# Seven block products in place of eight for the gate and up matmuls of a streaming encoder layer

## The chip, the cores and the metric

The kernel runs on one core of one Trainium2 chip, in one launch. The metric is the device time of that launch in microseconds. A core has a matrix engine (TensorE, PE in the profile, with its weight loads as PEld), a vector engine (VectorE, DVE), a scalar engine (ScalarE, ACT), a general engine (GpSimd, POOL) and a sync engine (SyncE, SP) that here issues the DMAs. Matmul results go to eight PSUM banks; everything else lies in on-chip memory of 128 partitions.

## The reference

One inference step of one layer with 1024 new tokens of a prompt and 32 tokens of a running stream, 1056 columns in all, model width 1024, feed-forward width 2816. Attention and retention come first; the part that this change touches is the second half:

```python
x = x + mix @ w_o
h = rmsnorm(x, g_ffn)
x = x + (jax.nn.silu(h @ w_ff_gate) * (h @ w_ff_up)) @ w_ff_down
gate = jax.nn.sigmoid(rmsnorm(x, g_ple) @ w_ple_gate)
return x + gate * (p @ w_ple)
```

All data is 32-bit float. Each matmul operand is split into two 16-bit halves (a high part and a rest), and a product is made of three 16-bit matmuls: high by high, high by rest, rest by high.

## The kernel before, in words

Tokens lie along the free dimension, channels along the partitions. The first stage (projections, attention, retention) is planned by hand (class Flow, line 80): a planner with a cost for each step and engine writes out the order. At its end it loads the weights of the output projection (`load_wo_0`, `load_wo_1`, lines 1216 and 1225) and of the last stage's `p @ w_ple` (`load_ple`, 1241), queued at lines 1347 to 1350.

From line 1390 on the order is not written out by hand. The build places each instruction in its engine's queue by dependences and estimated times, with a preference for what comes first in the program; on the chip each queue is then worked off in order. The stages are:

- **Output projection** (1432 to 1461): three token chunks of 352 (`CH`), eight output blocks of 128 channels each, 24 matmuls of 352 columns for each (`mm3`, lines 440 to 443: three matmuls for each of eight input blocks). DVE adds the old x (1451), SP stores it to DRAM (1453), ACT and DVE sum its squares (354). After a chunk `norm_steps` (319) queues three steps that run behind the next products: nothing, then four small matmuls with a power of -1/2 on POOL (333), then the broadcast matmul on PE (342) and the split of the normalized chunk into halves (347 to 352; every second subtraction is on POOL).
- **Gate and up** (1398 to 1430 and 1465 to 1511): 22 rows j of 128 feed-forward channels. `load_gu` brings the gate and the up weights of two rows (1 MB each), finds their largest magnitude (1406 on DVE, then `partition_all_reduce` on POOL, 285), derives a power-of-two scale, and splits them into halves (1410 on ACT, 1411 on DVE). `gu_mm` makes, for each row and each chunk of 352 tokens, a gate and an up product of 24 matmuls each. `gu_out` (1471) makes silu(gate) times up out of the two banks: tanh on ACT (1474), two DVE operations (1475, 1476), a 16-bit copy on ACT (1478), a DVE rest (1479). All 22 result rows stay on the chip in `aT` (1469).
- **Down** (1481 to 1561): eight output blocks m; `load_dn` loads and prepares the weights of one block (its maximum also goes through POOL, 1494), `down` makes 66 matmuls of 352 columns for each token chunk.
- **Last stage** (1564 to 1589): the second norm, the gate product and the output.

PSUM after line 1390: seven rotating banks for the products (`psb`) and one for the norms (`pss`). Weight tiles rotate through three buffers (`wpool`), staged weights through two (`stg`).

Of the kernel before, what the change touches and what calls it, by code (L numbers as in the profile page):

```python
# [33 lines left out]
NCH = 3  # L34
EPS = 1e-6
# [8 lines left out]
def _f(x):  # L44
    return float(x)
# [132 lines left out]
def kernel(  # L178
# [35 lines left out]
    mix_d = dram.tile([H, P, 2, T], F16, name="mix_d")  # L214

# [62 lines left out]
    def weight_scale(amax, n, gi, tag, pool=True, norm=False):  # L278
# [3 lines left out]
        if pool:  # L282
            yield G(0, 0.1)
            ar = sm(n, tag + "ar", 3)
            nc.gpsimd.partition_all_reduce(ar, amax, P, ABSMAX)  # L285
            yield from p2of(p2, ar, n, tag)
        else:
            ar = yield from spread_max(amax, n, tag)
            yield from p2of(p2, ar, n, tag, norm)
            yield ("put", "o")  # L290
# [4 lines left out]
        nc.vector.tensor_scalar(out=s, in0=s, scalar1=_f(2.0 ** -50) if norm else 16384.0, scalar2=None, op0=ALU.mult)  # L295
# [8 lines left out]
    def weight_scale_now(amax, n, gi, tag):  # L304
        g = weight_scale(amax, n, gi, tag)
# [13 lines left out]
    def norm_steps(acc, dg, tag, split, late=0):  # L319

        pending.extend([lambda: None] * late)
        B = CH // 4
        box = []

        def first():
            ps = pss.tile([P, 512], F32, tag="ss", name="ss")
            for b in range(4):
                nc.tensor.matmul(out=ps[0:B, CH + b:CH + b + 1], lhsT=acc[:, b * B:(b + 1) * B], rhs=ones32[:, 0:1],
                                 start=True, stop=True)
            v = sm(4, tag + "v")  # L330
            nc.vector.tensor_scalar(out=v[0:B], in0=ps[0:B, CH:CH + 4], scalar1=_f(1.0 / D), scalar2=EPS, op0=ALU.mult, op1=ALU.add)
# [8 lines left out]
        def second():  # L340
            ps, d = box
            nc.tensor.matmul(out=ps[:, 0:CH], lhsT=ones32[0:B], rhs=d[0:B], start=True, stop=True)
            split(ps[:, 0:CH])
# [10 lines left out]
    def square_sum(pool, xf, k0, k1, acc):  # L354

        for k in range(k0, k1):
            sq = acc if k == 0 else pool.tile([P, CH], F32, tag="sq", name="sq")
# [97 lines left out]
    with ExitStack() as pa:  # L455
# [83 lines left out]
        def const_b():  # L539
# [10 lines left out]
            yield ("delay", 2.0)  # L550

# [760 lines left out]
        def stream():  # L1312
# [10 lines left out]
            for s in range(NT * H + LAG):  # L1323
                at[0] = s
                h, i = divmod(s, NT)
                if h < H:
# [19 lines left out]
                    if i == 4 and h + 1 == H:  # L1346
                        flow.add(load_wo_0(), 0)
                        flow.add(load_ple(), 1)
# [49 lines left out]
    def load_gu(jp):  # L1398
        w = wtile()[:, 0:KD * 1024].rearrange("p (j u a k c) -> p j u a k c", j=2, u=2, a=2, k=KD)
        hds = []  # L1400
        for jj in range(2):
            j = 2 * jp + jj
            st = stage()[:, 0:KD * 256].rearrange("p (k u c) -> p k u c", k=KD, u=2)
            nc.sync.dma_start(out=st, in_=wgu[j])
            am = sm(2, "gam2", 3)
            nc.vector.tensor_reduce(out=am, in_=st.rearrange("p k g c -> p g k c"), axis=AX.XY, op=ALU.max,  # L1406
                                    apply_absolute_value=True)
            s, d = weight_scale_now(am, 2, 1, "gu")
            for u in range(2):
                nc.scalar.activation(w[:, jj, u, 0], st[:, :, u], AF.Copy, scale=s[:, u:u + 1])  # L1410
                nc.vector.scalar_tensor_tensor(out=w[:, jj, u, 1], in0=st[:, :, u], scalar=s[:, u:u + 1],
                                               in1=w[:, jj, u, 0], op0=ALU.mult, op1=ALU.subtract)

            nc.vector.tensor_scalar(out=rf[:, j:j + 1], in0=d[:, 0:1], scalar1=_f(2.0 ** 55), scalar2=d[:, 1:2],
                                    op0=ALU.mult, op1=ALU.mult)
            hd = sm(1, "hdg", 6)
            nc.vector.tensor_scalar(out=hd, in0=d[:, 0:1], scalar1=0.5, scalar2=None, op0=ALU.mult)
            hds.append(hd)
        return w, hds

    def gu_mm(wt, jj, c):
        cs = slice(c * CH, (c + 1) * CH)
        out = []
        for u in range(2):
            ps = bank()
            for k in range(KD):
# [262 lines left out]
```

## Time and profile before

| | before |
|---|---|
| time, median of 3 runs | 2012.23 us (2009.94 to 2014.46) |
| time of the profiled execution | 2011.19 us |
| its span, first to last instruction | 2009.2 us |
| PE busy | 1953.9 us, 97% |
| DVE busy | 1328.2 us, 66% |
| ACT busy | 925.7 us, 46% |
| POOL busy | 553.8 us, 28% |
| DMA | 137.52 MB, mean 68 GB/s |
| granted TensorE clock | 0.994 of full |

Times in the rows are microseconds from the first instruction unless they are marked as means in ns. Matmuls are pipelined: a row of 314 ns for one does not mean that the next starts 314 ns later. A row's last part says how long its engine was idle before it and which instruction ended that.

### The profile page before, as it was taken

To read this page: it belongs to the slowest core of one execution; us is meant where nothing else is said; L and a number is where in the kernel's file an instruction comes from. 1 tells how busy PE (TensorE), PEld (TensorE's weight loads), DVE (VectorE), ACT (ScalarE), POOL (GpSimd) and SP (SyncE) were. 2 spreads that over 40 slices of the span, in tenths; PEclk is the share of its full clock that TensorE was granted. 3 is DMA by queue.
4 is the path that set the end of the run, shared out by engine and by line. 5 is a ranking of instruction groups with operands and counts; after the bars stand their busy time and mean duration, and the time that the engine had idled before them with its cause. 6 is when DMAs were issued, how large, how long until landed. Compare 5 with 4: busy or idle time off the path is not lost.

```text
span 2009.2 us, 35867 instructions
## 1 busy us (share of the span) xinstructions
PE 1953.9 (97%) x13577; PEld 1204.5 (60%) x13577; DVE 1328.2 (66%) x3465; ACT 925.7 (46%) x2406; POOL 553.8 (28%) x1059
## 2 busy tenths in 40 slices
PE   5899999999999999999999999999999999999999
PEld 2465565655655555555565566666666666666665
DVE  6887878787777877877987666454445543543364
ACT  6676666666666666666665233222223221111132
POOL 4654445454453545444441011000000000000010
PEclk9999999999999999999999999999999999999999
DMA  5121202112021111211216431211111103111131
GB/s 190 69 71 51 80 25 65 54 52 67 26 74 57 47 62 32 75 59 28 81 32 243 160 118 46 81 43 42 43 43 53 49 29 116 58 58 43 43 123 51
DMA packets 67148, 137.52 MB, mean 68 GB/s; under 512 B 24832, under 2 KB 49536, under 8 KB 59040
## 3 DMA queue, kind: packets, MB, share of 16 engines
q1 hardware_dynamic: 66976, 135.25, 20.3%
q8 instruction: 106, 1.74, 0.4%
q14 instruction: 66, 0.54, 0.1%
HBM read 108.74 MB, written 26.48 MB: 67 GB/s over the span
## 4 chain that ended last, share of the span: by engine, by line
PE 81%; DVE 9%; ACT 3%; POOL 3%; DMA 2%; issue 1%; SPq 0%; POOLq 0%; ACTq 0%; DVEq 0%
PE ps L441 10%; PE ps L442 10%; PE ps L443 10%; PE pj L688 8%; PE pj L690 8%; PE pj L689 8%; PE ps L1522 4%; PE ps L1521 4%; PE ps L1520 4%; PE sc L825 2%; PE sc L828 1%; PE t L872 1%; PE pj L699 1%; PE t L1020 1%; ACT p L843 1%
## 5 line engine op out<-in xcount | busy, mean ns | idle before, releaser
L441 PE MATMUL ps<-mixs,w 128*128 128x352 f16 x1248 | 391.5, 314 | 1.5 <-DVE pws L1298 1.5
L689 PE MATMUL pj<-w,xh 128*128 128x512 f16 x1024 | 389.6, 381 | 3.1 <-DVE w L434 3.1
L688 PE MATMUL pj<-w,xh 128*128 128x512 f16 x1024 | 390.8, 382 | 1.8 <-ACT w L432 1.8
L442 PE MATMUL ps<-mixs,w 128*128 128x352 f16 x1248 | 391.3, 314 | 0.0
L443 PE MATMUL ps<-mixs,w 128*128 128x352 f16 x1248 | 391.2, 313 | 0.0
L690 PE MATMUL pj<-w,xh 128*128 128x512 f16 x1024 | 389.6, 380 | 0.0
L441 PEld LDWEIGHTS <-w 128*128 128x128 f16 x1488 | 146.3, 98 | 79.5 <-DVE pws L1298 1.9
L442 PEld LDWEIGHTS <-w 128*128 128x128 f16 x1488 | 146.1, 98 | 77.3 <-issue 1.3
L443 PEld LDWEIGHTS <-w 128*128 128x128 f16 x1488 | 146.1, 98 | 77.3
L690 PEld LDWEIGHTS <-xh 128*128 128x128 f16 x1024 | 100.5, 98 | 125.8 <-issue 6.1
L1522 PE MATMUL ps<-aT,w 128*128 128x352 f16 x528 | 165.0, 313 | 0.0
L1521 PE MATMUL ps<-aT,w 128*128 128x352 f16 x528 | 165.0, 313 | 0.0
L1520 PE MATMUL ps<-aT,w 128*128 128x352 f16 x528 | 165.0, 313 | 0.0
L843 ACT ACTIVATE p<-sc,nb,scs 128x256 f32<-128x256 f32 (+7 forms) x128 | 106.1, 829 | 99.4 <-POOL nb L837 66.4
L688 PEld LDWEIGHTS <-xh 128*128 128x128 f16 x1024 | 101.2, 99 | 72.6 <-issue 1.0
L689 PEld LDWEIGHTS <-xh 128*128 128x128 f16 x1024 | 100.6, 98 | 71.6 <-issue 2.9
L1478 ACT ACTIVATE aT<-th 128x352 f16<-128x352 f32 x66 | 32.5, 494 | 201.2 <-DVE th L1476 195.4
L835 DVE TENSOR_REDUCE nm<-sc 128x2 f32<-128x256 f32 (+6 forms) x112 | 102.8, 918 | 23.5 <-PE sc L828 23.2
L285 POOL PARTITION_ALL_REDUCE guar<-gam x22 | 8.9, 406 | 364.5 <-DVE gam L1406 351.6
L1476 DVE SCALAR_TENSOR_TENSOR th<-th,ps 128x352 f32<-128x352 f32 x66 | 34.3, 519 | 101.8 <-PE ps L443 101.7
L1475 DVE SCALAR_TENSOR_TENSOR th<-th,ps 128x352 f32<-128x352 f32 x66 | 34.2, 518 | 89.7 <-ACT th L1474 89.6
L1474 ACT ACTIVATE th<-ps,hdg 128x352 f32<-128x352 f32 x66 | 36.2, 550 | 114.1 <-PE ps L443 113.8
(400 smaller groups left out, 4209.5 us busy)
## 6 DMA issues: line engine op xcount, KB each, us to landing
st<-in_win_dram SPq DMA_DIRECT2D x30, 1024.0 KB, 4.9
st<-in_wgu_dram SPq DMA_DIRECT2D x22, 1024.0 KB, 5.1
st<-in_wdn_dram SPq DMA_DIRECT2D x16, 704.0 KB, 4.4
out_dram<-kv SPq DMA_DIRECT2D x64, 128.0 KB, 1.7
mixs<-mix_d SPq DMA_DIRECT2D x8, 528.0 KB, 6.8
pw_d<-pws SPq DMA_DIRECT2D x12, 352.0 KB, 3.6
xf<-in_xT_dram SPq DMA_DIRECT2D x3, 1408.0 KB, 7.2
x_d<-xf SPq DMA_DIRECT2D x24, 176.0 KB, 2.2
```

What stands on the lines that cost most here:

```text
L441: nc.tensor.matmul(out=ps, lhsT=wh, rhs=ah, start=first, stop=False)
L442: nc.tensor.matmul(out=ps, lhsT=wh, rhs=al, start=False, stop=False)
L443: nc.tensor.matmul(out=ps, lhsT=wl, rhs=ah, start=False, stop=last)
L688: nc.tensor.matmul(out=ps, lhsT=xhi, rhs=w[:, k, 0], start=(k == 0), stop=False)
L689: nc.tensor.matmul(out=ps, lhsT=xhi, rhs=w[:, k, 1], start=False, stop=False)
L690: nc.tensor.matmul(out=ps, lhsT=xh[:, k, 1, t0:t0 + P], rhs=w[:, k, 0], start=False, stop=(k == KD - 1))
L825: nc.tensor.matmul(out=o, lhsT=q4[:, m, 0:R], rhs=kts[:, m], start=True, stop=False)
L835: nc.vector.tensor_reduce(out=nm[0:R, mc], in_=pv, axis=AX.X, op=ALU.max, negate=True)
L843: nc.scalar.activation(pt[0:R, 0:NK], ps[0:R, p0:p0 + NK], AF.Exp, bias=nb[0:R, m:m + 1], scale=sc_ap[0:R], accum_out=Z[0:R, m:m + 1])
L1520: nc.tensor.matmul(out=ps, lhsT=wt[:, 0, j], rhs=aT[:, j, 0, cs], start=(j == 0), stop=False)
L1521: nc.tensor.matmul(out=ps, lhsT=wt[:, 1, j], rhs=aT[:, j, 0, cs], start=False, stop=False)
L1522: nc.tensor.matmul(out=ps, lhsT=wt[:, 2, j], rhs=aT[:, j, 1, cs], start=False, stop=(j == NF - 1))
```

## The change

For a pair of token blocks the gate and the up product of one row form a 2 by 2 block product: the weights are cut in two along the input channels (four 128-channel blocks each), the tokens are taken as two blocks of 264. A scheme of the Strassen and Winograd kind makes the four results from seven block products in place of eight. The parts:

- **Sizes.** Token blocks are 264 (`CW`), four of them (`NW`), in two pairs; output projection, norm, gate and up use them. Down and the last stage keep 352.
- **Weights** (`prep_gu`, one row at a time in place of two): the bound for the scale comes from two sums of squares on ACT; four sums or differences of weight quarters (512 columns) are made on POOL; seven operands are split into halves on ACT and DVE (one operation of 1024 columns and five of 512 on each). The scale still goes through `partition_all_reduce` on POOL.
- **Tokens** (`operands`, `sums`): after the norm of the second block of a pair, four groups of four sums on POOL each make the combined operands, which ACT and DVE split into halves.
- **Products** (`gu_pair`): seven products of 12 matmuls of 264 columns for each row and pair. Two go through an ACT copy; six DVE additions and one on POOL (`comb(q, u, q, on=nc.gpsimd)`) put the results together. Then `gu_out` as before for each of the two blocks, on 264 columns.
- **Order.** The first pair of rows 0 and 1 runs while the last norm is made. From row 2 on the weights of row j + 2 are prepared between the two pairs of row j.
- **Memory.** 14 of the 22 rows (`NS`) have a place on the chip through the stage; rows 0 to 7 are stored to DRAM (`a_d`) and use the places of later rows. After the stage two blocks of x and the eight rows are loaded (`back`). The down products of the blocks m = 0 and 1 are begun with rows 8 to 21 in six banks and ended with rows 0 to 7.
- **Loads at the end of the first stage.** `load_ple` is queued ahead of `load_wo_0`.
- Two small DVE operations rescale constants at the start.

```diff
+CW = 264
+NW = 4
+NS = 14
...
+    a_d = dram.tile([NF - NS, P, 2, T], F16, name="a_d")
...
-                        flow.add(load_wo_0(), 0)
-                        flow.add(load_ple(), 1)
+                        flow.add(load_ple(), 0)
+                        flow.add(load_wo_0(), 1)
...
+    def prep_gu(j, st):
+        wt = wtile()
+        w = wt[:, 0:7 * 2 * HK * P].rearrange("p (i a k c) -> p i a k c", i=7, a=2, k=HK)
+        tmp = wt[:, 7 * 2 * HK * P:7 * 2 * HK * P + 2 * HK * P].bitcast(F32).rearrange("p (k c) -> p k c", k=HK)
+        q1, q2, q3, q4 = (st[:, i * HK:(i + 1) * HK, u] for u in range(2) for i in range(2))
+        am2 = sm(2, "gam2", 3)
+        for i in range(2):
+            nc.scalar.activation(w[:, S3 + i].bitcast(BF16), st[:, i * HK:(i + 1) * HK].rearrange("p k u c -> p u k c"),
+                                 AF.Square, accum_out=am2[:, i:i + 1])
+        am = sm(1, "wam", 3)
+        nc.vector.tensor_tensor(out=am, in0=am2[:, 0:1], in1=am2[:, 1:2], op=ALU.max)
+        s, d = weight_scale_now(am, 1, 1, "gu", True)
+        def split(i, src, n=1):
+            src = src if n == 2 else src.unsqueeze(1)
+            nc.scalar.activation(w[:, i:i + n, 0], src, AF.Copy, scale=s)
+            nc.vector.scalar_tensor_tensor(out=w[:, i:i + n, 1], in0=src, scalar=s, in1=w[:, i:i + n, 0],
+                                           op0=ALU.mult, op1=ALU.subtract)
+        def comb(out, in0, in1, op):
+            nc.gpsimd.tensor_tensor(out=out, in0=in0, in1=in1, op=op)
+        comb(tmp, q1, q3, ALU.subtract)
+        comb(q3, q3, q4, ALU.add)
+        split(A1, st[:, :, 0].rearrange("p (i k) c -> p i k c", i=2), 2)
+        split(S1, q3)
+        comb(q1, q3, q1, ALU.subtract)
+        split(A4, q4)
+        comb(q2, q2, q1, ALU.subtract)
+        split(S3, tmp)
+        split(S2, q1)
+        split(S4, q2)
+        nc.vector.tensor_scalar(out=rf[:, j:j + 1], in0=d, scalar1=_f(2.0 ** 44), scalar2=d, op0=ALU.mult, op1=ALU.mult)
+        hd = sm(1, "hdg", 6)
+        nc.vector.tensor_scalar(out=hd, in0=d, scalar1=0.5, scalar2=None, op0=ALU.mult)
...
+            def gu_out(j, cs, hd, pg, pu):
+                th = tp.tile([P, CW], F32, tag="th", name="th", bufs=2)
+                nc.scalar.activation(th, pg, AF.Tanh, scale=hd)
+                nc.vector.scalar_tensor_tensor(out=th, in0=th, scalar=1.0, in1=pg, op0=ALU.add, op1=ALU.mult)
+                nc.vector.scalar_tensor_tensor(out=th, in0=th, scalar=_f(2.0 ** -34), in1=pu, op0=ALU.mult, op1=ALU.mult)
+                hi = a_row(j)[:, 0, cs]
+                nc.scalar.activation(hi, th, AF.Copy, scale=_f(2.0 ** -11))
+                nc.vector.scalar_tensor_tensor(out=a_row(j)[:, 1, cs], in0=hi, scalar=-2048.0, in1=th,
                                                op0=ALU.mult, op1=ALU.add)
...
+            def gu_pair(j, p, w, hd):
+                ca, cb = (slice((2 * p + i) * CW, (2 * p + i + 1) * CW) for i in range(2))
+                def prod(i, b):
+                    ps = bank_w()
+                    for k in range(HK):
+                        hi, lo = b(k)
+                        mm3(ps, w[:, i, 0, k], w[:, i, 1, k], hi, lo, k == 0, k == HK - 1)
+                    step()
+                    return ps
...
+                u = snapped(prod(A1, x(0, ca)))
+                q = snapped(prod(S1, x(0, cb)))
+                ga = snap()
+                comb(ga, u, prod(A2, x(HK, ca)))
+                comb(u, u, prod(S2, t(T2)))
+                comb(q, u, q, on=nc.gpsimd)
+                comb(u, u, prod(A4, t(T4)), ALU.subtract)
+                gb_ = snap()
+                comb(gb_, q, prod(S4, x(HK, cb)))
+                p7 = prod(S3, t(T3))
+                comb(u, u, p7)
+                comb(q, q, p7)
+                gu_out(j, ca, hd, ga, u)
+                gu_out(j, cb, hd, gb_, q)
...
+                    def sums(k):
+                        xa, t = xfs[c - 1], tT[p]
+                        a1, a3, b2, b4 = xa[:, k], xa[:, HK + k], xf[:, k], xf[:, HK + k]
+                        tt = nc.gpsimd.tensor_tensor
+                        tt(out=a1, in0=b2, in1=a1, op=ALU.subtract)
+                        parts16(place(HK + k), b4)
+                        tt(out=b2, in0=b4, in1=b2, op=ALU.subtract)
+                        parts16(place(k), a1)
+                        tt(out=b4, in0=b4, in1=a1, op=ALU.subtract)
+                        parts16((t[:, T3, k, 0], t[:, T3, k, 1]), b2)
+                        tt(out=a3, in0=b4, in1=a3, op=ALU.subtract)
+                        parts16((t[:, T2, k, 0], t[:, T2, k, 1]), b4)
+                        parts16((t[:, T4, k, 0], t[:, T4, k, 1]), a3)
+                    pending[0:0] = [lambda k=k: sums(k) for k in range(HK)]
...
+                for c in range(NW):
+                    c0 = c * CW
+                    xf = xc.tile([P, KD, CW], F32, tag="xf", name="xf")
+                    nc.sync.dma_start(out=xf, in_=xT[:, :, c0:c0 + CW])
+                    xfs.append(xf)
+                    acc = wk.tile([P, CW], F32, tag="acc", name="acc")
+                    if c == 2:
+                        sts[0] = stage_gu(0)
+                    for m in range(KD):
+                        if (c, m) == (2, 5):
+                            gus[0] = prep_gu(0, sts[0])
+                            sts[1] = stage_gu(1)
+                        if (c, m) == (3, 5):
+                            gus[1] = prep_gu(1, sts[1])
+                            sts[2] = stage_gu(2)
...
+                    norm_steps(acc, lambda: wk.tile([P, CW], F32, tag="dg", name="dg"), "nb",
+                               lambda rs, c=c, xf=xf: operands(c, xf, rs), 1, CW)
+                for j in range(2):
+                    gu_pair(j, 0, *gus[j])
+                while pending:
+                    step()
...
+            gus[2] = prep_gu(2, sts[2])
+            sts[3] = stage_gu(3)
+            for j in range(NF):
+                if j > 1:
+                    gu_pair(j, 0, *gus[j])
+                if 1 < j < NF - 1:
+                    nxt = j + 2
+                    if nxt < NF:
+                        gus[nxt] = prep_gu(nxt, sts[nxt])
+                        if nxt + 1 < NF:
+                            sts[nxt + 1] = stage_gu(nxt + 1)
+                        else:
+                            sd = stage_dn(0)
+                    else:
+                        dn0 = prep_dn(sd)
+                        sd = stage_dn(1)
+                gu_pair(j, 1, *gus[j])
+                if j == 1:
+                    gus[3] = prep_gu(3, sts[3])
+                    sts[4] = stage_gu(4)
+                if j < NF - NS:
+                    nc.sync.dma_start(out=a_d[j], in_=a_row(j))
...
+        back = [ap.tile([P, 2, T], F16, name="b%d" % j) for j in range(NF - NS)]
+        x2 = xh_pool.tile([P, KD, T], F32, tag="xh", name="x2")
+        for m in range(2):
+            nc.sync.dma_start(out=x2[:, m], in_=x1_d[m])
+        for j in range(NF - NS):
+            nc.sync.dma_start(out=back[j], in_=a_d[j])
...
+        dns = [dn0, prep_dn(sd)]
+        halves = {}
+        for m in range(2):
+            for c in range(NCH):
+                halves[m, c] = bank()
+                down_mm(halves[m, c], dns[m][0], range(NF - NS, NF), c, last=False)
+        sd = stage_dn(2)
+        nxt = prep_dn(sd)
+        for m in range(2):
+            for c in range(NCH):
+                down_mm(halves[m, c], dns[m][0], range(NF - NS), c, first=False)
...
```

## Prediction of the time, made before the changed kernel ran

> **What bounds the kernel now.** I read the busy times first, then the stages, then what PE waited for from the output projection on.
>
> ```profile
> PE 1953.9 (97%) x13577; PEld 1204.5 (60%) x13577; DVE 1328.2 (66%) x3465; ACT 925.7 (46%) x2406; POOL 553.8 (28%) x1059
> ```
> ```profile
> core 0: us, PE busy (x) PEld busy (x) DVE busy (x) ACT busy (x) POOL busy (x), PEclk, DMA share, GB/s
> ...
> 1104.00:1195.00 91.00, 85.47 (x562) 55.70 (x563) 55.59 (x110) 26.28 (x46) 11.85 (x14) 0.96 0.39 129
> 1195.00:1668.00 473.00, 469.91 (x3141) 307.71 (x3140) 233.66 (x430) 114.07 (x179) 12.44 (x26) 1.00 0.15 51
> ```
> ```profile
> PE ss L342 <- DVE dg L335: 7.8, 2, 4.7
> PE ps L441 <- DVE pws L1298: 1.5, 1, 1.5
> ```
>
> The second window is nearly all gate and up: PE works 469.9 of 473.0 us, DVE half the time, POOL 12.4 us. PE waits 9.3 us in all from there to the end. So fewer PE columns would show as time one for one, as long as nothing else becomes late.
>
> What a matmul costs is the distance of the starts, not the printed length:
>
> ```profile
> 1199.71 0.31 PE L441 MATMUL ps<-mixs,w 128*128 128x352 f16 x1
> ...
> 1202.69 0.31 PE L443 MATMUL ps<-mixs,w 128*128 128x352 f16 x1
> ```
> ```profile
> 606.03 0.22 PE L892 MATMUL po<-vh,aT 128*128 128x128 f16 x1
> ...
> 606.42 0.39 PE L895 MATMUL po<-vh,aT 128*128 128x128 f16 x4
> ```
> ```profile
> 621.19 0.27 PE L825 MATMUL sc<-kT,q 128*128 128x256 f16 x1
> 621.30 0.19 PE L827 MATMUL sc<-mneg,mrow 128*128 128x64 bf16 x1
> ```
>
> Twenty steps of 352 columns take 2.98 us, 149 ns each; seven steps of 128 columns 0.39 us, 56 ns each. Between them 264 columns cost 56 + 136 x 93/224 = 112.5 ns, and the 256-column step of 0.11 us lies on that line. A weight load takes 98 ns and starts with the matmul before it, so it stays hidden at this size:
>
> ```profile
> L442 PEld LDWEIGHTS <-w 128*128 128x128 f16 x1488 | 146.1, 98 | 77.3 <-issue 1.3
> ```
>
> **PE work.** Gate and up now: 22 rows x 6 products x 24 = 3168 matmuls x 149 = 472.0 us, 21.46 a row. After: 22 x 14 products x 12 = 3696 x 112.5 = 415.8 us, 18.9 a row, 1.35 a product. That is -56.2 us if PE stays the bound. The output projection goes from 576 x 149 = 85.8 to 768 x 112.5 = 86.4: +0.6.
>
> A rule of the Trainium skill speaks against the change here: "TensorE: Matmul & The Clock Gate", section "Back-to-back issue gap", gives 81 ns for 128 columns and 131 ns for 512 when each matmul brings its weight load. By that line 264 columns would cost about 99 and 352 about 110 ns (estimates from the page), and gate and up would grow by some 16 us; the rows above, also with a load for each matmul, contradict it, and they decide.
>
> **DVE and ACT.** They get more work for each row:
>
> ```profile
> L1411 DVE SCALAR_TENSOR_TENSOR w<-st,gus,w 128x1024 f16<-128x1024 f32 x44 | 55.6, 1280 | 6.3 <-ACT w L1410 6.3
> ...
> L1476 DVE SCALAR_TENSOR_TENSOR th<-th,ps 128x352 f32<-128x352 f32 x66 | 34.3, 519 | 101.8 <-PE ps L443 101.7
> ```
>
> The two rows give 0.42 us for 264 elements and 0.70 for 512. A row has 24 operations of 264 (10.1 us), the weight rests 1.28 + 5 x 0.70 = 4.8, and some seven small ones, about 1: 15.9 of 18.9 us. DVE alone is not the bound, but it has little left with which to catch up after a wait. ACT has fewer operations of the same sizes (two squares, the six splits of halves, eight of 264), so it isn't the bound either.
>
> **POOL is where I look for the time.** Two kinds of instruction share its queue: the all-reduce of a maximum (L285) and elementwise work.
>
> ```profile
> 1139.86 0.48 POOL L285 PARTITION_ALL_REDUCE guar<-gam  x1 [5.05 <-DVE gam L1406]
> 1148.00 1.05 POOL L333 TENSOR_TENSOR nbr<-nbv,neghalf 88x4 f32<-88x4 f32 x1 [7.65 <-issue]
> ...
> 1205.53 0.47 POOL L285 PARTITION_ALL_REDUCE guar<-gam  x1 [3.90 <-DVE gam L1406]
> 1213.06 1.05 POOL L333 TENSOR_TENSOR nbr<-nbv,neghalf 88x4 f32<-88x4 f32 x1 [7.06 <-DVE w L1411]
> 1221.12 0.67 POOL L285 PARTITION_ALL_REDUCE guar<-gam  x1 [7.00 <-DVE th L1475]
> 1228.76 3.28 POOL L352 TENSOR_TENSOR mixs<-sx,mixs 128x352 f16<-128x352 f32 x4 [6.98 <-PE ps L443]
> 1237.94 0.37 POOL L285 PARTITION_ALL_REDUCE guar<-gam  x1 [5.90 <-issue]
> ```
>
> Each time POOL goes from one kind to the other, either way, 5.9 to 7.7 us pass; four elementwise operations of one kind follow each other in 3.28 us without a gap. The engines named as releasers had long been done. What such a gap does to engines that wait in order is in the trace too:
>
> ```profile
> 1232.07 0.89 ACT L1478 ACTIVATE aT<-th 128x352 f16<-128x352 f32 x2 [5.77 <-POOL mixs L352]
> 1232.60 0.96 DVE L1479 SCALAR_TENSOR_TENSOR aT<-aT,th 128x352 f16<-128x352 f16 x2 [6.36 <-ACT aT L1478]
> ```
>
> ACT and DVE stood for about 6 us behind POOL. PE didn't notice, since seven banks at 24 x 0.149 = 3.6 us a product cover it. And the two PE waits at L342 are on a power of POOL behind such a gap (1148.00, 1213.06).
>
> After the change each row has one all-reduce (its weights) among elementwise work (four sums of 512, two q additions of 264). So POOL changes kind twice for every row, against nearly never now. I take 5.9 into the all-reduce (1237.94) and 7.0 back (1228.76): 12.9 us a row; bounds 11.8 (twice 5.9) to 15.3 (twice 7.65).
>
> The Trainium skill has this in "GPSIMD Engine Reference", section "2.1 Instruction dispatch": the first call to freshly loaded code pays about 6 us. By the page two changes would be 12.0 us, and the forecast below about 18 us lower; the measured gaps decide.
>
> ```profile
> L638 POOL TENSOR_TENSOR w<-w 128x1024 f32<-128x1024 f32 x7 | 16.7, 2383 | 11.8 <-ACT xsq L633 11.8
> ...
> L285 POOL PARTITION_ALL_REDUCE guar<-gam x22 | 8.9, 406 | 364.5 <-DVE gam L1406 351.6 <-DVE th L1475 7.0 <-issue 5.9
> ...
> L352 POOL TENSOR_TENSOR st<-sx,st 128x352 f16<-128x352 f32 x4 | 3.4, 853 | 7.3 <-ACT st L350 7.3
> ```
>
> On the line of 853 and 2383 ns, 264 elements cost 0.65 and 512 cost 1.22 us. POOL's own row is 2 x 0.65 + 4 x 1.22 + 0.41 + 12.9 = 19.5 us, already over PE's 18.9.
>
> **The loop.** The q addition ties the products to this queue: the next DVE step overwrites u, which q reads, and both later results of the pair need q. I expect this order on POOL, since the weights of row j + 2 become ready when the weight tile of row j - 1 is free, at the start of row j: two weight sums, all-reduce, q of the first pair, two weight sums, q of the second pair. From one first-pair q to the next:
> - DVE from that q to the u of the second pair: the six additions in between (6 x 0.42 = 2.5), and what else stands in DVE's queue there. I count three operations of one `gu_out` and two weight rests (1.26 + 1.40): 5.2 us. Bounds: 2.5 with none, 8.5 with both `gu_out`s (2.5) and all five rests of 512 (3.5). POOL's two other sums lie beside it.
> - q of the second pair 0.65, two sums 2.43, change 5.9, all-reduce 0.41, change 7.0, q 0.65.
> - Four hand-overs between engines, 0.5 in all (estimate: small beside the rest).
>
> That is 5.2 + 0.65 + 2.43 + 5.9 + 0.41 + 7.0 + 0.65 + 0.5 = 22.7 us a row. PE's 18.9 fits in it; while q is late, banks stay full, and seven banks cover 7 x 1.35 = 9.5 us, less than the two changes. Rows 0 and 1 run mostly outside the loop. Gate and up: 2 x 18.9 + 20 x 22.7 = 491.8, +19.8 us against 472.0.
>
> **Last norm to first rows: +10.** In POOL's queue the weight work of rows 1 and 2 (two pairs of changes, 25.8 us), the power (1.05) and 16 sums of 264 (10.4) stand together, 37 us, and PE has 14 products (18.9) to cover them: a stall of about 18 where 7.8 stand now. Bounds: -8 (all hidden, and the old waits gone) to +20.
>
> **To the down stage: +2.** SP's queue gets two blocks of x and eight rows, 10 x 528 KB, behind the last drains.
>
> ```profile
> x<-x_d SPq DMA_DIRECT2D x8, 528.0 KB, 7.4
> ```
> ```profile
> GB/s 190 69 71 51 80 25 65 54 52 67 26 74 57 47 62 32 75 59 28 81 32 243 160 118 46 81 43 42 43 43 53 49 29 116 58 58 43 43 123 51
> ```
>
> One after the other they would take 74 us, but the 22nd of 40 slices moved 243 GB/s, at which 5.4 MB take 22. The begun products cover 6 x 42 x 0.149 = 37.5 us. I charge 2 for the wait on the last row (0 to 36, the 74 less the cover). The stores of eight rows and the down weights behind them on SP have the whole stage.
>
> **At nothing:** the two small DVE operations at the start, and the swapped loads at the end of the first stage, where the second half of the output weights is first needed after four products, 10.8 us; if that cover is gone, a few us (bounds -3 to +3).
>
> **Sum**, on the profiled execution's own 2011.19 us (span 2009.2 and 2.0 around it, 0.05% under the median): +0.6 + 19.8 + 10 + 2 = +32.4, so **2044 us**.
>
> **The rivals.**
> - *PE keeps the bound (faster).* The banks and DVE's reserve take up the waits, and POOL's 19.5 us is all that a row costs: 2 x 18.9 + 20 x 19.5 = 427.8, -44.2, with +12.6 as above 1980 us; with all hidden, 2011.2 - 56.2 + 0.6 = 1956. It decides where the loop falls below 21 us a row, which needs DVE's stretch under 3.5 us. For it: the stretch must hold only 2.5, and the 6 us stand at 1232 cost PE nothing. Against: two such stands in each row, with banks filled 2.7 times as fast. Chance 0.33, of which 0.06 for 1956.
> - *Break-even.* Stretch near 3.5, loop near 21: 2 x 18.9 + 20 x 21 = 457.8, -14.2 + 12.6, 2010 us. Chance 0.12.
> - *The stretch is long.* 8.5 us: 26.0 a row, 557.8, +85.8 + 12.6, 2110 us. Chance 0.11.
> - *The matmuls don't shrink.* A fixed cost for each that the rows don't show would keep 264 near 149 ns: 3696 x 149 = 550.7, +79 with +12.6, 2103 us. The skill's line named above is a mild form of it. Against: the 56 and 110 ns rows. Chance 0.02.
>
> **How the numbers follow.** The forecast, 2020 to 2075, has 0.42. Slower by over 0.2% (about what a measurement of this kernel can tell from no change) takes that, the last two and 0.01 of break-even: 0.56. Faster: 0.33 and 0.04 of break-even, 0.37. Same: 0.07. The range 1968 to 2095 leaves out the fully hidden case, half of the long stretch and the tails, some 0.2.
>
> **What would show it.** Right: gate and up near 490 us at PE busy 85% or less; PE waiting for banks that DVE frees; DVE in front of u and q waiting for POOL; gaps of 6 to 7 us around every all-reduce, some 20 times; 264-column steps of 112 ns. Wrong: rows at 19 us with PE above 95% (the loads hidden), or PE waits named after DVE while POOL is idle (DVE is the bound).

## The result and the profile after

The changed kernel took 2088.6 us (median of 4 runs, 2085.32 to 2090.15) against 2012.43 beside it (4 runs): ratio 1.0377, 95% interval 1.0359 to 1.0395, so 76 us slower. The forecast was 2044, 32 us slower. The sign and the place were as forecast, and the mechanism in the main; the size was more than double. The profiled execution of the changed kernel took 2085.32 us, 74.1 over that of before.

Busy times of the whole execution:

```profile
PE 1937.1 (93%) x14307; PEld 1291.1 (62%) x14307; DVE 1479.6 (71%) x3955; ACT 1068.0 (51%) x2744; POOL 728.2 (35%) x1221
```

PE worked 17 us less than before and lost 4 points of its share. The next view cuts the time from the first matmul of the output projection to the first of the down stage (1104.2 to 1751.7; before, 1104.85 to 1678.91): the output projection, rows 0 and 1, rows 2 and 3, rows 4 to 19, rows 20 and 21. A row begins with the weight load of its first product.

```profile
core 0: us, PE busy (x) PEld busy (x) DVE busy (x) ACT busy (x) POOL busy (x), PEclk, DMA share, GB/s
1104.00:1207.00 103.00, 95.50 (x800) 80.36 (x800) 59.34 (x132) 35.89 (x83) 32.04 (x34) 0.93 0.31 105
1207.00:1274.00 67.00, 44.74 (x346) 35.88 (x344) 48.53 (x100) 28.81 (x62) 29.45 (x30) 0.80 0.12 42
1274.00:1332.00 58.00, 42.92 (x341) 35.07 (x340) 38.09 (x87) 26.15 (x49) 17.30 (x17) 0.88 0.16 56
1332.00:1714.00 382.00, 329.07 (x2690) 274.10 (x2688) 247.89 (x611) 178.03 (x353) 109.71 (x112) 0.93 0.15 51
1714.00:1752.00 38.00, 38.00 (x340) 32.98 (x338) 31.81 (x65) 13.00 (x27) 4.18 (x6) 1.00 0.20 60
```

The last line is what the change could do: two rows in 38.0 us with PE never idle, 18.9 a row, at full clock. In the line above it sixteen rows take 23.9 each, PE is idle 53 us and the granted clock is 0.93. No gate or up weights are left to prepare in rows 20 and 21. POOL still makes one all-reduce there, for the first down weights, with a change of kind before it, another behind it and a q addition behind that:

```profile
1729.29 0.41 POOL L291 PARTITION_ALL_REDUCE dnar<-dam  x1 [6.00 <-issue]
1736.88 0.73 POOL L1512 TENSOR_TENSOR sn<-sn 128x264 f32<-128x264 f32 x1 [7.17 <-DVE w L1636]
```

PE did not wait for it. One such turn in two rows was covered; what costs time in the rows before is that every row has one and each turn has to follow the one before. What PE waited for:

```profile
PE ps L448 <- DVE sn L1512: 72.9, 21, 6.5
PE ps L448 <- ACT sn L1508: 12.1, 1, 12.1
PE ss L335 <- DVE acc L367: 8.3, 2, 4.4
...
PE ps L448 <- ACT pws L1308: 4.9, 1, 4.9
PE ss L349 <- DVE dg L342: 4.3, 2, 3.4
```

The first line is the forecast's: PE waits for banks that the additions of `gu_pair` (L1512) empty. One turn of POOL's queue, all-reduce to all-reduce, is 23.87 us:

```profile
1460.54 0.41 POOL L291 PARTITION_ALL_REDUCE guar<-wam  x1 [5.88 <-issue]
1468.09 0.73 POOL L1512 TENSOR_TENSOR sn<-sn 128x264 f32<-128x264 f32 x1 [7.14 <-issue]
1468.80 2.61 POOL L1443 TENSOR_TENSOR st<-st 128x512 f32<-128x512 f32 x2
1475.18 1.27 POOL L1443 TENSOR_TENSOR w<-st 128x512 f32<-128x512 f32 x1 [3.78 <-PE ps L450]
1476.40 0.75 POOL L1512 TENSOR_TENSOR sn<-sn 128x264 f32<-128x264 f32 x1
1477.11 1.29 POOL L1443 TENSOR_TENSOR st<-st 128x512 f32<-128x512 f32 x1
1484.41 0.41 POOL L291 PARTITION_ALL_REDUCE guar<-wam  x1 [6.02 <-issue]
```

The q addition at 1468.09 is that of a second pair. Behind it VectorE and then PE go on:

```profile
1468.86 1.45 DVE L1512 TENSOR_TENSOR sn<-sn,ps 128x264 f32<-128x264 f32 x4 [2.65 <-POOL sn L1512]
1470.22 1.47 DVE L1482 SCALAR_TENSOR_TENSOR th<-th,sn 128x264 f32<-128x264 f32 x1
...
1484.86 0.15 DVE L229 TENSOR_SCALAR guc<-guar 128x1 f32<-128x1 f32 x1 [2.50 <-POOL guar L291]
```
```profile
1469.34 0.38 PE L448 MATMUL ps<-tT,w 128*128 128x264 f16 x1 [3.12 <-DVE sn L1512]
1469.51 0.42 PE L449 MATMUL ps<-tT,w 128*128 128x264 f16 x1
...
1472.37 0.36 PE L450 MATMUL ps<-mixs,w 128*128 128x264 f16 x1
1472.57 0.28 PE L448 MATMUL ps<-mixs,w 128*128 128x264 f16 x1
...
1474.94 0.28 PE L448 MATMUL ps<-mixs,w 128*128 128x264 f16 x1
```

PE has three products of that pair left. The first fifteen steps from one matmul to the next take 3.23 us, most of them 0.22 (the granted clock is 0.50 there), the others 0.112 each, so the next row's first product starts at 1474.94, 5.6 us after the wait. Then the row's weight tile is free, POOL writes a sum into it (1475.18, 3.78 us of waiting), and the next all-reduce can follow. So the loop closes through the weight tile: a change of kind, q, the rest of the products, three operations of POOL, a change of kind, the all-reduce.

### The profile page after: what moved, and what is told of

Read it like the earlier page. It is cut to its first block, busy times and chain, and to the rows that moved or that the text cites. A ratio compares the mean times of both kernels' runs of the same rounds, so it can differ in the third digit from the quotient of the medians.

```text
span 2083.5 us, 38669 instructions
## 1 busy us (share of the span) xinstructions
PE 1937.1 (93%) x14307; PEld 1291.1 (62%) x14307; DVE 1479.6 (71%) x3955; ACT 1068.0 (51%) x2744; POOL 728.2 (35%) x1221
## 4 chain that ended last, share of the span: by engine, by line
PE 63%; DVE 18%; issue 7%; POOL 6%; ACT 5%; DMA 0%; SPq 0%; POOLq 0%; ACTq 0%; DVEq 0%
PE pj L700 8%; PE pj L701 8%; PE pj L702 8%; PE ps L448 4%; PE ps L449 4%; PE ps L450 4%; PE ps L1678 4%; PE ps L1676 4%; PE ps L1677 4%; DVE w L1439 3%; DVE sn L1512 3%; PE sc L837 2%; PE sc L840 2%; PE t L884 1%; POOL sn L1512 1%
## 5 line engine op out<-in xcount | busy, mean ns | idle before, releaser
L448 PE MATMUL ps<-mixs,w 128*128 128x264 f16 x960 | 271.5, 283 | 17.4 <-ACT sn L1508 12.1
L449 PE MATMUL ps<-mixs,w 128*128 128x264 f16 x960 | 270.7, 282 | 0.0
L450 PE MATMUL ps<-mixs,w 128*128 128x264 f16 x960 | 269.9, 281 | 0.0
L449 PEld LDWEIGHTS <-w 128*128 128x128 f16 x1728 | 174.9, 101 | 134.8 <-issue 95.1
L448 PE MATMUL ps<-tT,w 128*128 128x264 f16 x528 | 157.2, 298 | 72.5 <-DVE sn L1512 72.5
L448 PEld LDWEIGHTS <-w 128*128 128x128 f16 x1728 | 175.3, 101 | 41.0 <-issue 0.2
L450 PEld LDWEIGHTS <-w 128*128 128x128 f16 x1728 | 175.2, 101 | 41.2
L1438 ACT ACTIVATE w<-st,gus 128x512 f16<-128x512 f32 (+1 forms) x110 | 84.2, 801 | 195.9 <-POOL st L1443 111.5
L1512 DVE TENSOR_TENSOR sn<-sn,ps 128x264 f32<-128x264 f32 x264 | 101.4, 423 | 96.3 <-POOL sn L1512 93.3
L450 PE MATMUL ps<-tT,w 128*128 128x264 f16 x528 | 158.1, 300 | 0.0
L449 PE MATMUL ps<-tT,w 128*128 128x264 f16 x528 | 157.9, 299 | 0.0
L847 DVE TENSOR_REDUCE nm<-sc 128x2 f32<-128x256 f32 (+6 forms) x112 | 102.8, 918 | 19.8 <-PE sc L840 19.4
L1439 DVE SCALAR_TENSOR_TENSOR w<-st,gus,w 128x512 f16<-128x512 f32 (+1 forms) x110 | 93.0, 877 | 23.6 <-ACT w L1438 23.6
L1678 PE MATMUL ps<-a,w 128*128 128x352 f16 x336 | 105.0, 312 | 1.3 <-DVE a L1485 1.3
L1676 PE MATMUL ps<-a,w 128*128 128x352 f16 x336 | 105.0, 312 | 0.0
```

The source lines that it names most:

```text
L448: nc.tensor.matmul(out=ps, lhsT=wh, rhs=ah, start=first, stop=False)
L449: nc.tensor.matmul(out=ps, lhsT=wh, rhs=al, start=False, stop=False)
L450: nc.tensor.matmul(out=ps, lhsT=wl, rhs=ah, start=False, stop=last)
L847: nc.vector.tensor_reduce(out=nm[0:R, mc], in_=pv, axis=AX.X, op=ALU.max, negate=True)
L1439: nc.vector.scalar_tensor_tensor(out=w[:, i:i + n, 1], in0=src, scalar=s, in1=w[:, i:i + n, 0], op0=ALU.mult, op1=ALU.subtract)
L1512: on.tensor_tensor(out=out, in0=in0, in1=in1, op=op)
```

## The experiments

Three theories were set against each other. L: POOL's change of kind, between the all-reduce and elementwise work, ties up the products, as forecast. D: VectorE is the bound. S: POOL's elementwise work is too slow by itself. The kernel before ran between 2010.9 and 2012.8 us (medians) beside all of them.

**The all-reduces of the later stages made without POOL** (a transpose on PE, a maximum on VectorE, a matmul by ones on PE), in the changed kernel and in the one before:

```diff
-            nc.gpsimd.partition_all_reduce(ar, amax, P, ABSMAX)
+            ar = yield from spread_max(amax, n, tag, True)
```

> The changed kernel with every all-reduce of a weight maximum after the first stage made by TensorE and VectorE (a transpose, a maximum, a product with ones) in place of POOL; POOL keeps its weight sums and the q additions. Theory L (POOL's change between all-reduce and elementwise work is the cost, 13 us a row): no gaps on POOL, rows fall from 23.9 to 18.9 to 19.5 us, the waits before the norms go, time 1955 to 1985 us. Rival D (VectorE is the bound; it gets 0.3 us more a row): rows stay above 22 us, time over 2045. Rival S (POOL's elementwise work of 6 us a row is too slow where it stands): rows of 21 or more, over 2030.

> The kernel before with the same replacement of the all-reduces after the first stage. Theory L: only the two waits of TensorE at the norms (7.8 us) go, rows stay at 21.5 us, time 2002 to 2006 us. Were the replacement itself slow or fast for another reason, the time would move by more than 10 us either way.

Measured 2073.1 us (ratio 1.0311, 1.0294 to 1.0329) and 2040.3 (1.0146, 1.0131 to 1.0161). Both missed. The replacement itself costs the kernel before 29 us, though PE waits little in its rows; most of it, 23 us, lies in the stretch of the down products, which grew from 237 to 260 us, with a wait of 11.7 us of PE for weights of the last stage. In the changed kernel PE's waits are:

```profile
PE mt L281 <- DVE gumc L273: 48.2, 21, 4.5
PE mt L270 <- DVE wam L414: 14.5, 3, 11.7
```

The ones-matmul waits in PE's queue for a maximum that stands in VectorE's queue, 21 times. One wait was traded for another, and the pair tells nothing about L.

**q on VectorE**: `comb(q, u, q)` in place of `on=nc.gpsimd`.

> The changed kernel with the one addition of a pair that stood on POOL (q = u + q) on VectorE; the all-reduce and the weight sums stay on POOL. If the tie of the products to POOL's queue by q is what makes the change of kind costly (theory L as I predicted it): POOL's row of 18 us runs beside the products, rows of 19 to 20.5 us, time 1990 to 2030. If POOL's queue holds the products by the weight sums as well (VectorE and ScalarE wait in order for them): rows of 22 or more, time over 2050. Rival D (VectorE is the bound; it gets 0.8 us a row): slower than the changed kernel.

Measured 2051.1 (1.0197, 1.0182 to 1.0212), 37 under the changed kernel: the second of the expected cases. POOL's queue still takes 23.3 us from all-reduce to all-reduce (1421.02 and 1444.36), 13.7 of them in the two changes. Whether the sums in that queue cost time only there, or do something else besides, the run alone doesn't say.

**One more change of kind each way in a row**: an unread all-reduce behind the first pair's `gb_`.

> The changed kernel with one more all-reduce on POOL in each row (of one column, behind the first pair's result, read by nobody), so that POOL changes kind four times a row in place of two. Theory L: rows grow by 11 to 14 us to 35 to 38 us, time 2290 to 2370 us. Rivals D and S: the all-reduce itself is 0.4 us, rows grow by less than 1 us, time under 2115.

Measured 2273.5 (one run), 185 more, 8.4 us for each of 22 rows. In the steady rows a turn takes 33.7 us (all-reduces at 1445.13 and 1478.86): the two new changes with their all-reduce add 13.6, and POOL's wait of 3.8 is gone. The way and the order of size are L's, but the time is 16 us under its range, since L had not counted with that wait.

**The same two changes where nothing waits for them**: in the kernel before, one unread addition of one column on POOL next to each row's all-reduce.

> The kernel before with one unread single-column addition on POOL beside each row's all-reduce: two changes of kind per row, and no product waits for any of them. L: the changes cost only what waits for them; 22 gaps each way of 6-7 us appear on POOL, the weights come some 13 us later but a row ahead of use, and the time stays within 2008-2020. If a change of kind slowed the chip otherwise (other engines, the DMA queues), 2030 or more.

```profile
1350.87 0.37 POOL L285 PARTITION_ALL_REDUCE guar<-gam  x1 [20.05 <-DVE gam L1406]
1357.91 0.18 POOL L1409 TENSOR_TENSOR xrg<-gam 128x1 f32<-128x1 f32 x1 [6.67 <-issue]
1364.00 0.37 POOL L285 PARTITION_ALL_REDUCE guar<-gam  x1 [5.90 <-issue]
1371.49 0.18 POOL L1409 TENSOR_TENSOR xrg<-gam 128x1 f32<-128x1 f32 x1 [7.12 <-issue]
```

The gaps are there, also around an addition of one column, and the time is 2016.6 (1.0024, 1.0015 to 1.0034): 5 us for 22 rows. So a change of kind costs little by itself; it costs what stands behind it.

**No search across the partitions**: a constant that lies in the same power of two takes the place of the all-reduce; the search is left out and no matmul replaces it.

```diff
+            if tag == "gu":
+                nc.vector.tensor_scalar(out=ar, in0=amax, scalar1=0.0, scalar2=1.15, op0=ALU.mult, op1=ALU.add)
...
```

In the kernel before the constant is 0.17.

> Left out: the search across the partitions for the gate/up scale; a VectorE operation writes the constant 1.15, which falls in the same power of two for all 22 rows of these inputs, so that the numbers stay the same. POOL's work in the rows is then of one kind, and no matmul is put in the place of the all-reduce. L (POOL's change of kind ties up the products): the rows fall from 23.9 to 18.9-19.6 us and the time to 1950-1980. D (VectorE the bound): rows of 20 or more with VectorE busy over 95%, 1985 or more. S (POOL's elementwise work too slow by itself): rows of 22 or more, 2030 or more.

> The kernel before without its search across the partitions in gate and up (a constant bound in the same power of two; left out: that search): the like of the fixed scale in the kernel before. Nothing in its rows waits for POOL but the norms behind the output projection (7.8 us in two waits). L: 2000-2012, so that the search cost the kernel before under 12 us where it cost the changed one 71.

Measured 2017.8 (1.0027, 1.0016 to 1.0038), 71 under the changed kernel, and 2001.6 for the kernel before (0.9951, 0.9935 to 0.9968), 11 under it. The search costs six times as much where products stand behind it. But 2017.8 is 38 over the range of L: the rows fell from 23.9 to 20.9 and not to 19. Rows and time fit D, but VectorE was busy for 83% (1332 to 1580), not for the 95 that D needs. S needed 2030 or more, and falls. What keeps them there stands in VectorE's and POOL's timelines of this kernel, one stretch of a row:

```profile
1440.35 0.42 DVE L1515 TENSOR_TENSOR sn<-sn,ps 128x264 f32<-128x264 f32 x1
1440.69 1.45 DVE L1484 SCALAR_TENSOR_TENSOR th<-th,sn 128x264 f32<-128x264 f32 x1
1442.06 1.23 DVE L1442 SCALAR_TENSOR_TENSOR w<-st,gus,w 128x512 f16<-128x512 f32 x1
1443.22 0.42 DVE L1515 TENSOR_TENSOR sn<-sn,ps 128x264 f32<-128x264 f32 x1
1443.56 1.41 DVE L1442 SCALAR_TENSOR_TENSOR w<-st,gus,w 128x512 f16<-128x512 f32 x1
1444.89 0.74 DVE L1442 SCALAR_TENSOR_TENSOR w<-w,gus 128x512 f16<-128x512 f32 x1
...
1447.24 0.42 DVE L1485 SCALAR_TENSOR_TENSOR th<-th,sn 128x264 f32<-128x264 f32 x1
```
```profile
1440.58 1.27 POOL L1446 TENSOR_TENSOR st<-st 128x512 f32<-128x512 f32 x1 [4.52 <-DVE w L1442]
1441.81 0.94 POOL L1515 TENSOR_TENSOR sn<-sn 128x264 f32<-128x264 f32 x1
1442.70 1.72 POOL L1446 TENSOR_TENSOR st<-st 128x512 f32<-128x512 f32 x1
```

The `th<-th,sn` of 1440.69 takes 1.45 us beside a POOL sum, that of 1447.24 takes 0.42 without one; a rest of 512 columns takes 1.23 and 1.41 beside one and 0.74 without. The addition with a PSUM operand at 1443.22 lies beside a POOL sum too and keeps its 0.42. From 1332 to 1580 there is no exception. All 47 `th<-th,sn` and rests that begin while a POOL addition runs are long (23 `th<-th,sn` of 1.44 to 1.51 us, 24 rests of 1.23 to 1.42). The 36 additions with a PSUM operand that do so take 0.42 to 0.43. And 11 `th<-th,sn` that began just before a POOL addition kept their 0.43. So a running POOL addition holds up a VectorE operation that begins behind it, where both of its operands come from the on-chip memory. The Trainium skill has this as a rule ("SBUF — State Buffer", section "Who interferes with whom"): a VectorE instruction with two SBUF inputs contends with a GpSimd instruction that reads SBUF, one with at most one SBUF input (outside the modes that use two ports) does not, and the order of issue decides which of the two is blocked. These counts agree. I called this H.

**A bound by PE without the all-reduce**: the squares of the partitions are added by a matmul by ones behind the fifth product of the first pair; then, with q on VectorE, behind the last.

```diff
+            nc.tensor.matmul(out=ps[:, 0:1], lhsT=ones32, rhs=am, start=True, stop=True)
```

> A real bound without the all-reduce: one matmul by ones adds the partitions' square sums (a bound that is looser by a few powers of two), and it is queued after the fifth product of the first pair, when the squares are long done, so that PE does not wait in order for them. L: as with the fixed scale plus under 0.5 us a row, 1955-1990, the row loop gone. Rival (what the earlier replacement by transpose and ones showed: PE's in-order wait for a value that is not ready): rows of 20.5-22, 2000-2040.

> The same without the constant: the partitions' square sums are added by two matmuls by ones, queued behind the last product of the first pair, where the squares should be done (with the matmul behind the fifth product PE waited 16 times, 27 us in all); q on VectorE, the weights' sums on POOL. If POOL's change of kind and what stands behind POOL's sums are all of the loss: rows of 18.9-19.5 and 1965-1990. If a bound through PE costs a wait in order wherever it is put: 27 us more than the kernel with the constant.

Measured 2023.5 (1.0052, 1.0037 to 1.0067) and 2021.5 (1.0048, 1.0033 to 1.0063). The first landed in its rival's range; the second missed the forecast's. It is 2 us from its like with the constant, next, so the bound by PE is nearly free there and the rest of the loss lies elsewhere.

**The constant and q on VectorE, then the weights' sums there too.** One edit lies between the two kernels, the engine of four sums a row.

> As the fixed scale (the search across the partitions left out, a constant bound in its place), and q on VectorE besides: the weights' sums stay on POOL, and no product's operand passes POOL any more. With the fixed scale alone 2.0 us of each row were left (20.9 in place of 18.9), and 2018. If these are products that stand behind the weights' sums in POOL's queue, the rows fall to 18.9-19.4 and the time to 1965-1985. If they are VectorE's in-order work (a split of the weights ahead of the products' additions), q there makes it no better: rows of 20.5 or more, 2005 or more.

> The constant bound (the search across the partitions left out), q and the weights' sums all on VectorE: POOL does nothing in the rows. Against the kernel with the constant and q on VectorE (2019) one thing differs, the engine of the weights' four sums. H (a POOL sum holds up every VectorE operation that reads two SBUF operands: such operations took 0.43 us alone and 1.45 beside a POOL sum, some 3.3 us a row): the long operations vanish, rows of 18.9-19.7, 1972-1985, although VectorE has four more sums of 0.68 each. Rival (the two us a row are VectorE's own work in order): 2.7 us more work a row makes it slower than 2019.

Measured 2019.3 (1.0041, 1.0026 to 1.0056) and 1971.7 (0.9805, 0.9787 to 0.9823). With the first one my reading of the constant's rows fell: products behind the sums in POOL's queue were not it, for q left that queue and nothing was won. The second landed where H had it, a little under its range. Below are the same stretch of both (behind its length the busy times of PE, PEld, VectorE, ACT and POOL) and one operation (its mean in ns stands behind its busy time), first with the sums on POOL:

```profile
1332.00:1580.00 248.00, 224.23 (x1948) 190.11 (x1947) 222.93 (x478) 128.09 (x255) 65.34 (x47) 1.00 0.16 57
```
```profile
L1485 DVE SCALAR_TENSOR_TENSOR th<-th,sn 128x264 f32<-128x264 f32 x46 | 29.6, 684 | 0.0
```

and with the sums on VectorE:

```profile
1332.00:1580.00 248.00, 247.00 (x2166) 211.52 (x2165) 224.51 (x580) 139.96 (x283) 0.00 (x0) 1.00 0.17 59
```
```profile
L1485 DVE SCALAR_TENSOR_TENSOR th<-th,sn 128x264 f32<-128x264 f32 x52 | 21.1, 426 | 0.0
```

VectorE is busy for the same 90% in both and does 580 operations in place of 478, since the time for which it is held counts as busy. In the first kernel 47 held operations take 49 us more than their like that aren't held, 4.2 us a row; the four sums add 2.7 a row to VectorE in the second. Rows went from 21.3 to 19.3 us, and 48 us of the whole time with them. The edit also takes away the hand-overs of the sums from POOL to ACT (14.6 us of ACT's waits in this stretch); what these are worth by themselves wasn't separated.

**All of POOL's additions in the rows to VectorE, the all-reduce kept on POOL.** This computes all that the changed kernel does; the tokens' sums, ahead of row 2, stay on POOL.

```diff
-            nc.gpsimd.tensor_tensor(out=out, in0=in0, in1=in1, op=op)
+            nc.vector.tensor_tensor(out=out, in0=in0, in1=in1, op=op)
...
-                comb(q, u, q, on=nc.gpsimd)
+                comb(q, u, q)
```

> The change with q and the weight sums on VectorE: POOL keeps only all-reduces in the rows. VectorE's work rises from about 15.9 to about 19 us a row (four sums of 512 columns at some 0.6, two of 264 at 0.36). L: the POOL gaps go; what is left is VectorE's wait for the all-reduce itself (2-3 us) with the second pair's operations behind it: rows of 19.5-22, 1975-2040. D: rows at VectorE's busy time, 20 or more, VectorE over 93% busy in the rows.

Measured 1980.9 (0.9841, 0.9826 to 0.9856): 108 under the changed kernel and 31 under the one before, the fastest with the search in it. Rows 2 to 7 take 18.9 us, rows 8 to 18 19.6 to 20.0. D falls with it, for VectorE has more work here than in the changed kernel:

```profile
1332.00:1580.00 248.00, 244.77 (x2136) 208.50 (x2134) 217.41 (x557) 136.44 (x278) 4.62 (x13) 1.00 0.18 63
```

Four of the kernels now make a square. With neither the search nor the rows' additions on POOL the time is 1971.7, with the search alone 1980.9, with the additions alone 2017.8, with both 2088.6. The search alone adds 9 us, the additions alone 46, both together 117. So some 62 us come only when the two share POOL's queue, and only then does POOL change kind in the rows. Most of the 46 goes with the weights' sums, where H lies.

**Only the weights' sums to VectorE, q and the all-reduce on POOL.**

> The change with only the weights' four sums on VectorE: the all-reduce and q stay on POOL, so a row still has one change of kind each way with products' operands behind it, but no POOL sum to hold VectorE's operations. L (the changes of kind bound the loop: 7.1 back, q 0.7, some 7 for PE's products from q to q, 0.7, 6.0 into the all-reduce, 0.4): rows of 21-23, 2020-2060. Rival (the hold of VectorE by POOL's sums is the greater part of the loss): rows below 20, under 2000.

Measured 2012.1 (1.0003, 0.9992 to 1.0014), 8 us under L's range. POOL's queue shows why the row is still 20.91 us, from all-reduce to all-reduce:

```profile
1452.62 0.41 POOL L291 PARTITION_ALL_REDUCE guar<-wam  x1 [6.03 <-DVE wam L1433]
1460.20 1.23 POOL L1512 TENSOR_TENSOR sn<-sn 128x264 f32<-128x264 f32 x1 [7.17 <-DVE w L1439]
1466.84 0.74 POOL L1512 TENSOR_TENSOR sn<-sn 128x264 f32<-128x264 f32 x1 [5.41 <-DVE sn L1512]
1473.53 0.41 POOL L291 PARTITION_ALL_REDUCE guar<-wam  x1 [5.95 <-DVE wam L1433]
```

0.41 + 7.17 + 1.23 + 5.41 + 0.74 + 5.95 = 20.91: two changes of kind and the products from one q to the other; that middle part is 5.4 and not the 7 that I had put there. Since the long operations of VectorE are nearly all gone here too, this run alone doesn't divide the gain between the shorter queue and H.

**The two loads at the end of the first stage put back**, in the fastest version.

> The change with q and the weights' sums on VectorE (1980.9), and the two loads at the end of the first stage put back in the order of the kernel before: what the swap is worth by itself. In the kernel with the swap PE waits 4.9 us for the output projection's weights. Theory: the swap costs what this wait shows, and the time falls by 2-5 us, to 1976-1979. Rival: the order of two loads only moves the wait to another step, within 1 us of 1980.9.

Measured 1980.8 (0.9845, 0.9831 to 0.9860), the same: the wait of 4.9 us fell to 1.5, but the first matmul of the output projection comes at 1106.10 where it came at 1105.94. Other work ahead of it takes the time that the wait took. The rival was right.

## Why the prediction was right in kind and short in size

**Right.** PE's work per row is 18.9 us (rows 20 and 21). The loop through POOL bounds the other rows. From the output projection to the end of gate and up there are 47 gaps: 24 into an all-reduce (22 of them 5.75 to 6.28 us) and 23 back (6.65 to 7.72). I had taken 5.9 and 7.0, and the turn above shows 6.02 and 7.14. The Trainium skill ("GPSIMD Engine Reference", section "2.1 Instruction dispatch") gives about 6 us for a first call after new code is loaded; here a gap of that size stands at every change in either direction, and the way back takes a microsecond more. Whether the gap is such a load no run here shows. The down stage was forecast at +2, and its stretch to the end went from 330.3 to 331.8 us; the first stage and the swapped loads were at nothing, -0.7 measured. The matmuls did shrink to 112 ns.

**The terms that were mis-sized.** From the output projection's first matmul to the down stage the forecast's own sum gives 574.06 + 0.6 + 10 + 19.8 = 604.5 us; it took 647.5. The 43 us lie in four places:

- *Output projection and rows 0 and 1*: 574.06 - 472.0 + 0.6 + 10 + 37.8 = 150.46 forecast, 169.84 measured, +19.4. The step "last norm to first rows: +10" failed: it came to 29.4, outside its own bounds of -8 to +20. The queue on POOL that it put at 37 us was 48.1 long (1202.2 to 1250.3). The four changes took 26.1, as forecast, but the all-reduces, the weights' sums and a q weren't in the sum (7.0 in all), and the 16 sums of the tokens took 14.0 in place of 10.4. PE's waits up to row 2 add up to 29.6 us where the forecast had 18, so 11.6 of the 19.4 are waits. The other 8 were not divided; the pace after the waits, which had no term, is in them (the granted clock was 0.80 from 1207 to 1274). With the search left out row 2 began 18.6 us earlier after the start of the output projection. That is about the stall of 18 which the forecast had put down to the changes; what it missed came on top of them.
- *Rows 2 and 3*: 45.4 forecast, 57.7 measured, +12.3. They were priced as two turns of the steady loop, but three lie in them (all-reduces at 1274.47, 1289.79 and 1317.92, of rows 3, 4 and 5).
- *Rows 4 to 19*: 22.7 forecast, 23.88 measured, +18.8 over sixteen rows. The loop was the right one with a wrong part in it. I put the first pair's q behind the all-reduce and let 5.2 us of VectorE's other work close the loop. The second pair's q stands there, and what closes it is PE: 6.36 us from the end of that q to the weight tile coming free, of which 5.6 are three products that start at half pace. Against 5.2 and 0.5 of hand-overs that is 0.66 more in the turn shown; the changes add 0.26, POOL's own operations 0.2. That a stretch of VectorE put at 5.2 was in truth one of PE of nearly the same length is luck.
- *Rows 20 and 21*: priced at 22.7, they have no gate and up weights to prepare and one turn between them, and took 37.9 in all: -7.5. This error has the other sign and hides a part of the rest.

Together 19.4 + 12.3 + 18.8 - 7.5 = 43.0.

**The rivals.** "PE keeps the bound" stood at 1980 on the thought that banks and VectorE's reserve would take up POOL's delays. In the changed kernel they didn't. 1980.9 comes out when POOL's additions leave the rows; it is another kernel, and that the two figures agree is chance. It shows the gain that the block products hold with the search in place, about 31 us. The forecast did not have H at all. In the turn of the changed kernel shown above it is off the loop: the held operation at 1470.22 makes no wait of PE. It became the next bound when the changes were gone (2018 and 2019, in place of 1972).

**Left open.** Why the rows of the fastest version go from 18.9 to 19.6 us at row 8 wasn't tried. More than three weight tiles, which would open the loop at another place, weren't tried either. How much of the 76 us at `weight_sums_on_dve` is H was not separated.

## What to carry to other kernels

Before giving an idle engine new work in the main loop, look at what else its queue holds: an engine that is 28% busy became the bound because two kinds of instruction alternate on it and each change costs 6 to 7 us with operands behind it, in every row. Price such a loop by walking it once through every queue and buffer, with the pace that the matmul engine has after a wait, and price the start of a stage as its own case, with every operation that stands in the queue, not as a few rows of the steady state. When a bound is taken away and the gain falls short, compare the length of the same operation in both traces: the next bound may be an engine that looks busy while it is held.

## What the runs showed of the hardware

- In the changed kernel POOL needs 5.75 to 6.28 us from elementwise work into an all-reduce (two of 24 gaps were longer, 7.61 and 7.75) and 6.65 to 7.72 back, each time. In the kernel before an added addition of one column had such gaps too (6.67 and 7.12).
- In the kernel with the constant bound, VectorE operations with two on-chip operands that begin while a POOL addition runs take 1.44 to 1.51 us in place of 0.42 at 264 columns, and 1.23 to 1.42 in place of 0.74 at 512. Those with a PSUM operand stay at 0.42 to 0.43, and so do those that began before the POOL addition.
- After a wait of 3.12 us the first fifteen steps of the 264-column matmuls took 3.23 us, most of them 0.22, then 0.112 each. After each of the 16 such waits in rows 4 to 19 (2.83 to 3.79 us) 12 to 16 steps were slow, behind one of 3.50 us at 1283.20 none; over these rows the granted clock was 0.93.
